# A decoder trunk on one core: a planner sets the order on every engine, transposing transfers replace some of TensorE's transposes, and four more blocks per MLP layer use seven products

## The chip, the core and the metric

The kernel runs on one core of a Trainium2 chip. The core has engines with queues of their own, each served in order: TensorE (PE) multiplies matrices, VectorE (DVE), ScalarE (ACT) and GpSimd (POOL) work elementwise, SyncE (SP) issues most transfers. An instruction waits on semaphores for what it reads and for the buffer that it writes. The metric is device time in microseconds of one execution, as the median of several runs.

## The reference

Two layers on x of 256 tokens by 2048 features, all in float32: a retention layer, then a latent-attention (MLA) layer, each followed by a squared-ReLU MLP. Cut to what matters:

```python
def retention(h, w_in, w_out, cos, sin):            # 8 heads, q and k of 256, v and gate of 512 each
    q, k, v, gate = split(h @ w_in)
    ...                                             # rotary q, k; decayed scores and state; per-head norm of o
    return (jax.nn.silu(gate) * o) @ w_out

def sq_relu_mlp(h, w1, w2):                         # w1 2048 x 8192, w2 8192 x 2048
    return jnp.square(jax.nn.relu(h @ w1)) @ w2

for layer in range(2):
    h = rms_norm(x, norm_mix[layer])
    x = x + (retention(h, ...) if layer == 0 else mla_attention(h, ...))
    x = x + sq_relu_mlp(rms_norm(x, norm_mlp[layer]), mlp_w1[layer], mlp_w2[layer])
```

## The kernel before

**Three products for one.** PE multiplies in a fast format that keeps fewer bits than float32. So each operand is split into a high part (ACT casts, line 216) and a low part (DVE subtracts, line 217), and a product is three matmuls: high by high, high by low, low by high (lines 409 to 411), each 128x512.

**Blocks.** Weights come as blocks of 256 rows by 1024 columns, 1 MB each, named *raw*, with three buffers; SP issues a load when DVE has finished with the buffer (line 324). The parts go to the buffers *wh* and *wl* of 1024 columns, five of each. A plain block takes eight products. A block "by seven" takes seven, in the manner of Strassen: DVE makes three sums of the weights (lines 363, 372, 373) and ACT and DVE split these too; the activations' sums are made once per block of activations (`with_sums`). Which of a pair's eight blocks go by seven is a tuple in the code:

```python
SEVEN, LATE, ODD, HEAD = (3, 5, 7), (5, 7), (1, 3, 5, 7), (2, 4, 6, 7)
```

**Pairs and groups.** A "pair" (`gemm_pair`) is eight blocks against the same 1024 output columns. An MLP layer is four groups; a group is two pairs of W1 (p = 2g and 2g + 1) and two pairs of W2. In the trace u is W1's product and d is W2's. At the end of a W1 pair, `pair_out` copies the sums out of PSUM (ACT, line 432; DVE, lines 434 to 439), `summed` adds (line 448), ACT applies ReLU with the norm (line 877), and the result, tokens by features, must be turned to features by tokens for W2. PE does that by eight 128x128 transposes for each half of the pair against the identity in *cst* (line 235, *hid_tp*); ACT squares what comes out (line 886), and ACT and DVE split it. The retention layer turns each head's gated output y in the same way (*ytp*).

**What sets the order.** The Python code records instructions in an order written out by hand: a queue of deferred functions (`later`, counted in blocks) puts the turning of a pair among the blocks of the next. Manual rules (`queued_behind`) hold single DVE or POOL instructions behind others. Products of W2's earlier groups are added to x in HBM by accumulating transfers from POOL (`to_home`, line 152).

Of the kernel before, what the change touches and what calls it, by code (L numbers as in the profile page):

```python
# [14 lines left out]
I32 = mybir.dt.int32  # L15
AF = mybir.ActivationFunctionType
# [3 lines left out]


# [24 lines left out]
GROUPS = (4, 4, 4, 4)  # L46
SEVEN, LATE, ODD, HEAD = (3, 5, 7), (5, 7), (1, 3, 5, 7), (2, 4, 6, 7)
# [19 lines left out]
def yoco(ctx: ExitStack, tc: tile.TileContext, a):  # L67
    nc = tc.nc
# [3 lines left out]
    def f2k(shape, name, dtype=F32):  # L72
        return pool.tile([P, *shape], dtype, tag="f2k", bufs=14, name=name)

    def small(w, name):
        return pool.tile([P, w], F32, tag="small", bufs=36, name=name)
# [5 lines left out]
    def bank(tag, shape, name):  # L82
        t = psum.tile([P, 512], F32, tag=tag, bufs=4 if tag == "acc" else 2, name=name)
        return shaped(t, shape)

    def two_banks(name):
        return psum.tile([P, 2, 512], F32, tag="at", bufs=1, name=name)

    def act_tile(name, dtype=F32R):

        return pool.tile([P, 2, 2, S], dtype, tag="act", bufs=24, name=name)


    queue, low_part, first_low = [], [None], [None]
    clock, count, ahead = [0], itertools.count(), [None, None]
# [19 lines left out]
    gains = pool.tile([P, G_ALL], F32, name="gains")  # L115
    cst = pool.tile([P, C_ALL], F32, name="cst")
    pos_i = pool.tile([P, NT], I32, name="pos_i")
    gpe = pool.tile([P, 2 * ROPE], F32, name="gpe")
# [3 lines left out]
    neg_half = pool.tile([P, 16], F32, name="neg_half")  # L122
# [4 lines left out]
    zeros = pool.tile([P, 512], BF16, tag="junk", bufs=1, name="zeros")  # L127
# [6 lines left out]
    x_home = [[dram.tile([P, 512], F32, name=f"xh_{t}_{b}") for b in range(NB)] for t in range(NT)]  # L134
# [14 lines left out]
    def to_home(c, p):  # L149

        def send(t, j, i):
            ins = nc.gpsimd.dma_start(x_home[t][2 * p + j], c[t][j][i], accum_op=ALU.add)
            tc.add_manual_dep(
                ins.ins, low_part[0].ins.name,
                mybir.DependencyInfo(mybir.DependencyClass.Sync, mybir.DependencyReason.SCHED_ONLY), reason="spaced",
            )
# [8 lines left out]
    def sums_into_x(c, name):  # L165
# [6 lines left out]
        queued_behind(nc.vector.tensor_tensor(v, c["p6"], o["p1"], op=ALU.add), low_part[0])  # L172
        nc.vector.tensor_tensor(u, c["p7"], v, op=ALU.add)

        def join(*parts):
            for t, j, part, op in parts:
                queued_behind(nc.vector.tensor_tensor(x[t][j], x[t][j], part, op=op), low_part[0])
# [31 lines left out]
    def square_sum(src, acc, name):  # L209
        junk = pool.tile([P, 512], BF16, tag="junk", bufs=1, name=f"{name}_sq")  # L210
# [26 lines left out]

    def stream(w, chunk, cols, name, use, done=None, before=None):

        raw = pool.tile([P, 2048], F32, tag="raw", bufs=3, name=f"{name}_raw")  # L240
# [3 lines left out]
        for half in range(2):  # L244
            wh = pool.tile([P, 1024], F32R, tag="wh", bufs=5, name=f"{name}_wh{half}")
            wl = pool.tile([P, 1024], F32R, tag="wl", bufs=5, name=f"{name}_wl{half}")
# [68 lines left out]
    def queued_behind(ins, before):  # L315
        tc.add_manual_dep(
            ins.ins, before.ins.name,
            mybir.DependencyInfo(mybir.DependencyClass.NoSync, mybir.DependencyReason.DATA), reason="order",
        )

    def quad(w, chunk, x, mm, name, split_ends=False):

        raw = pool.tile([P, 2048], F32, tag="raw", bufs=3, name=f"{name}_raw")
# [9 lines left out]
        def parts(src, n, part, after=None):  # L333
            wh = pool.tile([P, 1024], F32R, tag="wh", bufs=5, name=f"{name}_wh{part}")
            wl = pool.tile([P, 1024], F32R, tag="wl", bufs=5, name=f"{name}_wl{part}")
            low = low_part[0] = split(wh[:, : n * 512], wl[:, : n * 512], src)
            if after is not None:
                queued_behind(low, after)
            if part == 0:
                first_low[0] = low  # L340
# [21 lines left out]
        u = [pool.tile([P, 2, 512], F32, tag="us", bufs=2, name=f"{name}_u{i}") for i in range(2)]  # L362
        first_sum = nc.vector.tensor_tensor(
# [3 lines left out]
        if first_low[0] is not None:  # L367
            queued_behind(first_sum, first_low[0])
        if ahead[1] is not None:
            queued_behind(first_sum, ahead[1])  # L370
            ahead[1] = None
        nc.vector.tensor_tensor(u[1][:, 0], u[0][:, 0], raw[:, 512:1024], op=ALU.add)
        summed_up = nc.vector.tensor_tensor(u[1][:, 1], u[1][:, 0], raw[:, 1536:], op=ALU.add)  # L373
        b11, b22 = parts(raw[:, 0:1024], 2, 0, summed_up)
        mm("p1", a(0, 0), b11)
        mm("c12", s(3), b22)
        (b21,) = parts(raw[:, 1536:], 1, 1, summed_up)
# [156 lines left out]
    def add_to_x(acc, b, ss, name):  # L534
        for t in range(NT):
            for part in acc[t] if isinstance(acc[t], tuple) else (acc[t],):
                added = nc.vector.tensor_tensor(x[t][b], part, x[t][b], op=ALU.add)
                if name == "n2" and b >= 2:
                    queued_behind(added, low_part[0])
# [19 lines left out]
    pos_f = pool.tile([P, NT], F32, name="pos_f")  # L559
# [733 lines left out]
```

## Time and profile before

| | us |
|---|---|
| median of 3 runs | 2460.17 (2459.62 to 2461.29) |
| span of the profiled execution, its own time | 2456.3 |
| PE busy | 2446.2 |
| DVE busy | 2212.2 |
| ACT busy | 1641.3 |
| POOL busy | 238.0 |

The profile records one execution, and its span runs from the first to the last instruction. The time of a run also holds what lies around the span. Matmuls overlap in the records (a 128x512 matmul is recorded as 389 ns and starts every 227 ns), so PE's busy time is read as "was anything running", and what a matmul costs is read from the distance of starts. A group row reads: line, engine, operation, what it writes and reads, count | busy us, mean ns | idle time just before, and what ended it.

### The profile page before, as it was taken

The page shows a single profiled execution, that of the slowest core. Times are in us where ns is not written, and L with a number is a line of the kernel's source. Part 1 is how long each engine was busy: PE and PEld are TensorE (multiplying, and loading weights), DVE is VectorE, ACT ScalarE, POOL GpSimd, SP SyncE. Part 2 cuts the span into 40 slices and gives each one's busy share as a digit, 9 for nine tenths or more (in the row PEclk, how much of TensorE's full clock was granted, in tenths as well). Part 3 has the DMA queues.
Part 4 walks back from the last instruction along what each step waited for, and adds up shares of the span by engine and source line. Part 5 has one row for each costly group of instructions (what it writes and reads, how often), then busy time and mean ns, then how long its engine had stood idle before and what let it go on. Part 6 is the DMA issues. An engine that isn't in the chain of part 4 may idle for free.

```text
span 2456.3 us, 31721 instructions
## 1 busy us (share of the span) xinstructions
PE 2446.2 (100%) x11614; PEld 2057.6 (84%) x11614; DVE 2212.2 (90%) x2919; ACT 1641.3 (67%) x2307; POOL 238.0 (10%) x287
## 2 busy tenths in 40 slices
PE   9999999999999999999999999999999999999999
PEld 7888888888888888888888888998888888888887
DVE  7899899888899999999999998777899999999998
ACT  6566666556676767667676777577667667676674
POOL 6400001000000010010110001101000100100100
PEclk9999999999999999999999999999999999999999
DMA  8555569556565586695786555444555865957854
GB/s 309 207 201 191 192 202 259 191 183 224 197 218 194 196 254 218 207 272 187 241 253 213 200 202 180 155 162 173 197 199 205 252 228 194 262 198 229 264 209 170
DMA packets 93692, 521.05 MB, mean 212 GB/s; under 512 B 11104, under 2 KB 12512, under 8 KB 40288
## 3 DMA queue, kind: packets, MB, share of 16 engines
q1 hardware_dynamic: 72144, 472.83, 55.2%
q0 software_dynamic: 21248, 46.15, 8.9%
q8 instruction: 91, 1.49, 0.2%
q14 instruction: 65, 0.53, 0.1%
q10 hardware_dynamic: 144, 0.05, 0.0%
HBM read 479.14 MB, written 39.85 MB: 211 GB/s over the span
## 4 chain that ended last, share of the span: by engine, by line
PE 92%; DVE 2%; ACT 1%; issue 0%; DMA 0%; POOL 0%; ACTq 0%; DVEq 0%
PE u_c L411 7%; PE u_c L410 7%; PE u_c L409 7%; PE d_c L411 6%; PE d_c L410 6%; PE d_c L409 6%; PE rp_c L411 3%; PE rp_c L409 3%; PE rp_c L410 3%; PE u_p L411 2%; PE u_p L410 2%; PE u_p L409 2%; PE rq_acc L307 2%; PE rk_acc L307 2%; PE ro_c L411 2%; PE ro_c L409 2%
## 5 line engine op out<-in xcount | busy, mean ns | idle before, releaser
L217 DVE TENSOR_TENSOR d_wl<-d_raw,d_wh 128x1024 fp32r<-128x1024 f32 (+1 forms) x256 | 278.7, 1111 | 31.6 <-ACT d_wh L216 31.6
L217 DVE TENSOR_TENSOR u_wl<-u_raw,u_wh 128x1024 fp32r<-128x1024 f32 (+1 forms) x256 | 279.3, 1113 | 29.8 <-ACT u_wh L216 29.8
L409 PE MATMUL u_c<-u_wh,n 128*128 128x512 f32 x712 | 278.3, 392 | 0.0
L411 PE MATMUL u_c<-u_wh,n 128*128 128x512 f32 x712 | 277.2, 389 | 0.0
L410 PE MATMUL u_c<-u_wl,n 128*128 128x512 f32 x712 | 277.2, 389 | 0.0
L409 PE MATMUL d_c<-d_wh,hid 128*128 128x512 f32 x706 | 275.4, 392 | 0.5 <-ACT d_wh L216 0.5
L411 PE MATMUL d_c<-d_wh,hid 128*128 128x512 f32 x706 | 275.0, 390 | 0.0
L410 PE MATMUL d_c<-d_wl,hid 128*128 128x512 f32 x706 | 274.8, 389 | 0.0
L216 ACT CAST u_wh<-u_raw 128x1024 fp32r<-128x1024 f32 (+1 forms) x256 | 241.3, 973 | 49.6 <-PE u_c L411 24.1
L216 ACT CAST d_wh<-d_raw 128x1024 fp32r<-128x1024 f32 (+1 forms) x256 | 240.3, 971 | 39.9 <-PE d_c L411 16.6
L216 ACT CAST d_wh<-d_u 128x1024 fp32r<-128x1024 f32 x106 | 108.1, 1051 | 119.7 <-DVE d_u L373 82.6
L216 ACT CAST u_wh<-u_u 128x1024 fp32r<-128x1024 f32 x104 | 106.2, 1052 | 116.0 <-DVE u_u L373 77.3
L411 PEld LDWEIGHTS u_c<-u_wh,n 128*128 128x128 f32 x712 | 133.7, 188 | 27.8
L410 PEld LDWEIGHTS u_c<-u_wl,n 128*128 128x128 f32 x712 | 133.8, 188 | 27.4 <-DVE u_wl L217 0.3
L409 PEld LDWEIGHTS u_c<-u_wh,n 128*128 128x128 f32 x712 | 133.7, 188 | 27.0
L409 PEld LDWEIGHTS d_c<-d_wh,hid 128*128 128x128 f32 x706 | 132.6, 188 | 28.2 <-ACT d_wh L216 1.4
L411 PEld LDWEIGHTS d_c<-d_wh,hid 128*128 128x128 f32 x706 | 132.5, 188 | 27.6
L410 PEld LDWEIGHTS d_c<-d_wl,hid 128*128 128x128 f32 x706 | 132.6, 188 | 27.5 <-DVE d_wl L217 0.4
L216 ACT CAST rp_wh<-rp_raw 128x1024 fp32r<-128x1024 f32 x112 | 103.8, 945 | 74.2 <-PE rp_c L411 49.2
L217 DVE TENSOR_TENSOR rp_wl<-rp_raw,rp_wh 128x1024 fp32r<-128x1024 f32 x112 | 119.7, 1090 | 16.4 <-ACT rp_wh L216 16.2
L217 DVE TENSOR_TENSOR u_wl<-u_u,u_wh 128x1024 fp32r<-128x1024 f32 x104 | 123.5, 1222 | 3.1 <-ACT u_wh L216 2.8
L217 DVE TENSOR_TENSOR d_wl<-d_u,d_wh 128x1024 fp32r<-128x1024 f32 x106 | 125.8, 1221 | 0.0
(570 smaller groups left out, 6505.3 us busy)
## 6 DMA issues: line engine op xcount, KB each, us to landing
u_raw<-in_mlp_w SPq DMA_DIRECT2D x128, 1024.0 KB, 5.4
d_raw<-in_mlp_w SPq DMA_DIRECT2D x128, 1024.0 KB, 4.9
rp_raw<-in_ret_w_gv SPq DMA_DIRECT2D x56, 1024.0 KB, 4.8
ro_raw<-in_ret_w_out SPq DMA_DIRECT2D x32, 1024.0 KB, 4.9
uq_raw<-in_mla_w_uq SPq DMA_DIRECT2D x24, 768.0 KB, 4.3
rq_raw<-in_ret_w_qk SPq DMA_DIRECT2D x16, 1024.0 KB, 4.9
rk_raw<-in_ret_w_qk SPq DMA_DIRECT2D x16, 1024.0 KB, 4.8
xh<-d_c POOLq DMA_DIRECT2D x48, 256.0 KB, 6.1
```

Of the source, the lines that this page charges most:

```text
L216: nc.scalar.copy(h, src)
L217: return nc.vector.tensor_tensor(l, src, h.bitcast(F32), op=ALU.subtract)
L307: nc.tensor.matmul(acc[f], wh[:, cols], a.rearrange("p i s -> p (i s)"), start=k == 0, stop=k == nk - 1)
L409: nc.tensor.matmul(dst, ah, bh, start=n == 0, stop=False)
L410: nc.tensor.matmul(dst, ah, bl, start=False, stop=False)
L411: nc.tensor.matmul(dst, al, bh, start=False, stop=n == total[key] - 1)
```

## The change

**The order.** `nc` is no longer the real engine interface but a `Plan`: calls are recorded, with their buffers as index sets, and nothing is emitted. At the end `emit` runs `schedule`, a list scheduler. It gives each recorded instruction a cost from tables in the code, a due time from what depends on it, and then plays the engines forward: of the instructions that are ready on an engine, the one with the earliest due time goes next. Buffer slots are handed out in that play too. The instructions are emitted in that order, on all five engines. All `queued_behind` rules go.

**The turning.** For the first pair of each two (even p) and for seven of eight heads' y, PE no longer transposes. ACT copies each float32 tile into two 16-bit halves (`_h`), SP issues four transposing transfers of 128 x 512 halves, and ACT writes the halves back interleaved (`joined`) before squaring and splitting as before. The second pair (odd p) and head 7 are still turned on PE.

**The blocks.** W1's odd pairs take four of eight blocks by seven (ODD), where they took three (SEVEN). The other tuples are as they were.

The diff, cut to its core:

```diff
--- before.py
+++ after.py
...
+class Plan:
+
+    ENGINES = {"tensor": "PE", "vector": "DVE", "scalar": "ACT", "gpsimd": "POOL", "sync": "SP"}
+    LATENCY = {"PE": 55, "DVE": 36, "ACT": 48, "POOL": 110, "SP": 60}
...
+        op.engine, op.method, op.args, op.kw = self.ENGINES[engine], (engine, method), args, kw
+        op.number, op.before, op.after, op.new = len(self.ops), {}, [], []
+        op.made = op.held = None
+        op.behind, op.ahead = set(), []
...
+    def time(self, op, outs, ins):
+        engine, (_, method) = op.engine, op.method
+        n = max(v.index.size for v in outs if isinstance(v, View)) if any(isinstance(v, View) for v in outs) else 0
+        m = max([n] + [v.index.size for v in ins])
+        op.moves = None
+        if "dma" in method:
+            size = max(n, m) * P * (2 if "transpose" in method else 4)
+            issue = {"SP": 380, "ACT": 100, "POOL": 870}[engine]
+            if "transpose" in method:
+                issue = 1290
+            rate, wait = (208, 3200) if op.kw.get("accum_op") is not None else (349, 3000 if engine == "POOL" else 1800)
...
+            if "transpose" in method:
+                rate, wait = 180, 2200
+            op.moves = (size / rate, wait)
+            return issue, issue
...
+            if not op.after:
+                op.due = -whole
...
+            at, e = best
+            if not ready[e]:
+                while waiting[e] and waiting[e][0][0] <= at:
+                    _, _, op = heapq.heappop(waiting[e])
+                    heapq.heappush(ready[e], (op.due, op.number, op))
+            _, _, op = heapq.heappop(ready[e])
...
+        order = self.schedule()
+        with self.tc.manual_schedule(engines=engines):
+            for op in order:
+                engine, method = op.method
+                fn = getattr(getattr(self.nc, engine), method)
+                op.made = fn(*(real(v) for v in op.args), **{k: real(v) for k, v in op.kw.items()})
...
+TURNED_Y = 7
+STEPS = (((3,3,4),(3,4,5)),(None,None))
+TURNS = ((0,1),(0,1))
...
-    nc = tc.nc
+    nc = Plan(tc.nc, tc)
...
+    def halves_of(v):
+        return v.bitcast(U16).rearrange("p (n two) -> p two n", two=2)
+
+    def turn_by_dma(blocks, name, steps, then):
+
+        parts = [f2k([2, 512], f"{name}_h{t}", U16) for t in range(NT)]
+        for t in range(NT):
+            nc.scalar.copy(parts[t], halves_of(blocks[t]))
+
+        def turn():
+            turned = [f2k([4, S], f"{name}_t{i}", U16) for i in range(2)]
+            for t in range(NT):
+                for i in range(2):
+                    nc.sync.dma_start_transpose(turned[i][:, :, t * P : (t + 1) * P], parts[t][:, i])
+            for k2 in range(2):
+                later(steps[1 + k2] - steps[0], lambda k2=k2: then(turned, k2))
+
+        later(steps[0], turn)
+
+    def joined(turned, k2, u):
+
+        for i in range(2):
+            dst = halves_of(u.rearrange("p j s -> p (j s)"))[:, i]
+            part = nc.scalar.copy(dst, turned[i][:, 2 * k2 : 2 * k2 + 2].rearrange("p j s -> p (j s)"))
...
-                if ahead[0] is not None:
-                    queued_behind(low_part[0], ahead[0])
-                    ahead[0] = None
...
-    def queued_behind(ins, before):
-        tc.add_manual_dep(
-            ins.ins, before.ins.name,
-            mybir.DependencyInfo(mybir.DependencyClass.NoSync, mybir.DependencyReason.DATA), reason="order",
-        )
...
+            y_act.append((yt, with_sums(src, f"y{h}{k2}") if summed_up else None))
+
+        def join(turned, k2):
+            u = f2k([2, S], f"yu{h}{k2}")
+            joined(turned, k2, u)
+            split_up(k2, u)
+
         def turn():
+            if h < TURNED_Y:
+                turn_by_dma(ys, f"y{h}", (3,5,7), join)
+                return
             for k2 in range(2):
                 tp = transposed(lambda t, j: ys[t][:, (2 * k2 + j) * P : (2 * k2 + j + 1) * P], f"ytp{h}{k2}")
-                yt = act_tile(f"y{h}{k2}")
-                more = None
-                if len(y_act) in (HEAD if h < RH // 2 else LATE):
-                    u = f2k([2, S], f"yu{h}{k2}")
-                    nc.scalar.copy(u, tp)
-                    split_act(yt, u)
-                    more = with_sums(u, f"y{h}{k2}")
-                else:
-                    split_act(yt, tp)
-                y_act.append((yt, more))
+                u = f2k([2, S], f"yu{h}{k2}")
+                nc.scalar.copy(u, tp)
+                split_up(k2, u)
 
         later(2 if h else 3, turn)
 
...
         w1, w2 = a[f"mlp_w1_{layer}"], a[f"mlp_w2_{layer}"]
         f0 = 0
         for gi, nf in enumerate(GROUPS):
-            hid, blocks = [], []
+            blocks = []
             last = gi == len(GROUPS) - 1
 
-            def up(c, p, hid=hid, blocks=blocks):
+            def up(c, p, blocks=blocks):
 
                 need(r, NT)
                 c = summed(c)
-                for t in range(NT):
-                    for i in range(2):
-                        nc.scalar.activation(c[t][i], c[t][i], AF.Relu, scale=r[t])
-
-                def turn(i):
-                    for q in (2 * i, 2 * i + 1):
-                        name = f"hid{layer}_{p}{q}"
-                        tp = transposed(
-                            lambda t, j: c[t][q // 2][:, (q % 2 * 2 + j) * P : (q % 2 * 2 + j + 1) * P], f"{name}_tp"
-                        )
+
+                def turn_on_pe(i):
+                    for k2 in range(2):
+                        name = f"hid{layer}_{p}{2 * i + k2}"
+                        tp = transposed(lambda t, j: c[t][i][:, (k2 * 2 + j) * P : (k2 * 2 + j + 1) * P], f"{name}_tp")
                         u = f2k([2, S], f"{name}_u")
                         nc.scalar.activation(u, tp, AF.Square)
-                        v = act_tile(name)
-                        split_act(v, u)
-                        blocks.append((v, with_sums(u, name) if len(blocks) in ODD else None))
-                        hid.append(v)
-
-                later(0, lambda: turn(0))
-                later(1, lambda: turn(1))
+                        split_up(u, name)
+
+                def turn(i):
+                    for t in range(NT):
+                        nc.scalar.activation(c[t][i], c[t][i], AF.Relu, scale=r[t])
+                    steps = STEPS[p % 2][i]
+                    if steps is None:
+                        turn_on_pe(i)
+                        return
+                    turn_by_dma(
+                        [c[t][i] for t in range(NT)], f"hid{layer}_{p}{i}", steps,
+                        lambda turned, k2: square(turned, i, k2),
+                    )
+
+                def square(turned, i, k2):
+                    name = f"hid{layer}_{p}{2 * i + k2}"
+                    u = f2k([2, S], f"{name}_u")
+                    joined(turned, k2, u)
+                    nc.scalar.activation(u, u, AF.Square)
+                    split_up(u, name)
+
+                def split_up(u, name):
+                    v = act_tile(name)
+                    split_act(v, u)
+                    entry = [v, None]
+                    blocks.append(entry)
+                    if len(blocks) - 1 in ODD:
+                        later(0.5, lambda: entry.__setitem__(1, with_sums(u, name)))
+
+                for i in range(2):
+                    later(TURNS[p % 2][i], lambda i=i: turn(i))
 
             for p in range(f0 // 2, (f0 + nf) // 2):
-                seven = SEVEN if p % 2 else ODD if p else LATE
+                seven = (ODD, ODD)[p % 2] if p else LATE
                 gemm_pair(
                     w1, p * 8, act, [i in seven for i in range(8)], f"u{layer}_{p}", lambda c, p=p, up=up: up(c, p)
                 )
@@ -917,7 +1355,7 @@
                 def add(c, p=p, last=last):
                     into_x(done, c, p, 1) if last else to_home(c, p)
 
-                kinds = [i in ((LATE if last else ODD) if p else SEVEN) for i in range(2 * nf)]
+                kinds = [i in ((LATE if last else (SEVEN, ODD)[1]) if p else (SEVEN, ODD)[0]) for i in range(2 * nf)]
                 gemm_pair(w2, p * 32 + 2 * f0, blocks, kinds, f"d{layer}_{gi}{p}", add)
             f0 += nf
 
...
+    nc.emit()
```

What the planner does with this is seen in the engines' queues. In names, u0_31 is layer 0, W1 pair 3, block 1; u0_2 is what pair 2 left; hid0_20 is the first block of hidden activations of pair 2; the last number is a buffer's.

PE, at the boundary of the first and second block of W1's pair 3 in layer 0. Before, with the first half of pair 2 turned there:

```order
L409 MATMUL u0_3_c22_8495<-u0_30_wh1_8499,n116_00_6305 128x512
L410 MATMUL u0_3_c22_8495<-u0_30_wl1_8500,n116_00_6305 128x512
L411 MATMUL u0_3_c22_8495<-u0_30_wh1_8499,n116_00_6305 128x512
L235 MATMUL hid0_20_tp_8525<-cst_62,u0_2_c11_8464 128x128
L235 MATMUL hid0_20_tp_8525<-cst_62,u0_2_c21_8466 128x128
L235 MATMUL hid0_20_tp_8525<-cst_62,u0_2_c11_8464 128x128
L235 MATMUL hid0_20_tp_8525<-cst_62,u0_2_c21_8466 128x128
L235 MATMUL hid0_21_tp_8535<-cst_62,u0_2_c11_8464 128x128
L235 MATMUL hid0_21_tp_8535<-cst_62,u0_2_c21_8466 128x128
```

In the changed kernel:

```order
L421 MATMUL u0_3_c22_8568<-u0_30_wh1_8518,n116_00_6380 128x512
L421 MATMUL u0_3_c22_8568<-u0_30_wl1_8532,n116_00_6380 128x512
L421 MATMUL u0_3_c22_8568<-u0_30_wh1_8518,n116_00_6380 128x512
L421 MATMUL u0_3_p1_8598<-u0_31_wh0_8539,n116_01_6404 128x512
L421 MATMUL u0_3_p1_8598<-u0_31_wl0_8551,n116_01_6404 128x512
L421 MATMUL u0_3_p1_8598<-u0_31_wh0_8539,n116_01_6404 128x512
L421 MATMUL u0_3_c12_8562<-u0_31_wh0_8539,n101_more_6462 128x512
L421 MATMUL u0_3_c12_8562<-u0_31_wl0_8551,n101_more_6462 128x512
L421 MATMUL u0_3_c12_8562<-u0_31_wh0_8539,n101_more_6462 128x512
```

The eight transposes (two tiles of four) are gone, and block 1 starts with the product p1 of a block by seven, where it started with c11 of a plain one.

ACT, in blocks 3 to 5 of the same pair of the changed kernel, from the ReLU of pair 2's first half to the first copies out of its turned halves (`_wh` are casts of weights, `_t0` the turned 16-bit tile):

```order
L421 ACTIVATE u0_2_c21_8529<-u0_2_c21_8529,n1_r_6870 128x512
L421 COPY hid0_20_h0_8679<-u0_2_c11_8524 128x1024
L421 COPY hid0_20_h1_8687<-u0_2_c21_8529 128x1024
L421 CAST u0_34_wh0_8697<-u0_34_raw_8575 128x1024
L421 CAST u0_34_wh1_8706<-u0_34_raw_8575 128x1024
L421 CAST u0_35_wh0_8718<-u0_35_raw_8639 128x1024
L421 CAST u0_35_wh1_8726<-u0_35_raw_8639 128x512
L421 COPY hid0_20_u_8741<-hid0_20_t0_8690 128x512
L421 COPY hid0_21_u_8747<-hid0_20_t0_8690 128x512
L421 CAST u0_35_wh2_8754<-u0_35_u1_8708 128x1024
L421 CAST u0_35_wh3_8764<-u0_35_u0_8692 128x1024
L421 COPY hid0_20_u_8741<-hid0_20_t1_8715 128x512
```

Before, ACT took the turned tile from PSUM with one squaring instruction for each block:

```order
L877 ACTIVATE u0_2_c22_8460<-u0_2_c22_8460,n1_r_6762 128x512
L886 ACTIVATE hid0_20_u_8530<-hid0_20_tp_8525 128x512
L886 ACTIVATE hid0_21_u_8540<-hid0_21_tp_8535 128x512
L216 CAST hid0_20_8532<-hid0_20_u_8530 128x2x256
L216 CAST hid0_21_8542<-hid0_21_u_8540 128x2x256
```

The two 16-bit copies and four copies back are new; four casts of weights stand between the last 16-bit copy and the first copy back.

SP, in the same place of the changed kernel:

```order
L421 DMA u0_35_raw_8639<-in_mlp_w1_0 128x2048
L421 DMA u0_36_raw_8657<-in_mlp_w1_0 128x2048
L421 DMA_TRANSPOSE hid0_20_t0_8690<-hid0_20_h0_8679 128x4x128
L421 DMA_TRANSPOSE hid0_20_t0_8690<-hid0_20_h1_8687 128x4x128
L421 DMA_TRANSPOSE hid0_20_t1_8715<-hid0_20_h0_8679 128x4x128
L421 DMA_TRANSPOSE hid0_20_t1_8715<-hid0_20_h1_8687 128x4x128
L421 DMA u0_37_raw_8738<-in_mlp_w1_0 128x2048
L421 DMA d0_100_raw_8759<-in_mlp_w2_0 128x2048
L421 DMA d0_101_raw_8820<-in_mlp_w2_0 128x2048
```

Before, the same loads followed each other:

```order
L324 DMA u0_35_raw_8728<-in_mlp_w1_0 128x2048
L324 DMA u0_36_raw_8772<-in_mlp_w1_0 128x2048
L324 DMA u0_37_raw_8806<-in_mlp_w1_0 128x2048
L324 DMA d0_100_raw_8866<-in_mlp_w2_0 128x2048
L324 DMA d0_101_raw_8941<-in_mlp_w2_0 128x2048
```

Four transposing transfers now stand between the loads of blocks 6 and 7.

At the start of the program SP's first transfer was of the activations; in the changed kernel it is that of the constants (*cst*, 128x672), which stood fifteenth:

```order
L421 DMA cst_69<-in_cst 128x672
L421 DMA rg00_raw_73<-in_ret_w_gv0 128x512
L421 DMA x0t_0_77<-in_xt 128x256
L421 DMA rg00_raw_73<-in_ret_w_gv0 128x512
L421 DMA x0t_0_77<-in_xt 128x256
```

Before:

```order
L648 DMA x0t_0_99<-in_xt 128x256
L253 DMA rg00_raw_105<-in_ret_w_gv0 128x512
L656 DMA x0t_0_99<-in_xt 128x256
L253 DMA rg00_raw_105<-in_ret_w_gv0 128x512 x2
L654 DMA x0t_1_135<-in_xt 128x512
```

The loads of the first weights and activations now stand behind it.

More of the change, by code (lines that the diff above doesn't have):

```diff
@@ L331, in s, with parts @@
             return [more[:, n // 2, i, n % 2 * P : (n % 2 + 1) * P] for i in range(2)]
[L333 to L340, printed above, removed]
+        def parts(src, n, part):
+            wh = nc.tile(pool, [P, 1024], F32R, f"{name}_wh{part}", "wh", 5)
+            wl = nc.tile(pool, [P, 1024], F32R, f"{name}_wl{part}", "wl", 5)
+            low_part[0] = split(wh[:, : n * 512], wl[:, : n * 512], src)
             return [[i[:, j * 512 : (j + 1) * 512] for i in (wh, wl)] for j in range(n)]
```

437 lines of the change are left out of this document (378 added, 59 removed).

## The prediction

> **What bounds the kernel now.** I read the page first: the span, the engines' busy times and the shares of the chain that ended last.
>
> ```profile
> span 2456.3 us, 31721 instructions
> PE 2446.2 (100%) x11614; PEld 2057.6 (84%) x11614; DVE 2212.2 (90%) x2919; ACT 1641.3 (67%) x2307; POOL 238.0 (10%) x287
> PE 92%; DVE 2%; ACT 1%; issue 0%; DMA 0%; POOL 0%; ACTq 0%; DVEq 0%
> ```
>
> TensorE (PE) is busy for all but 2456.3 - 2446.2 = 10.1 us and carries 92% of the chain. VectorE (DVE) is second, 90%. The table of stretches then says where PE's idle time lies, and what DVE has left; its columns are stretch, length, and busy time with instructions of PE, PEld, DVE, ACT and POOL, then clock, DMA share and GB/s.
>
> ```profile
> 0.00:20.00 20.00, 17.88 (x65) 11.45 (x66) 11.63 (x23) 13.15 (x24) 2.06 (x8) 1.00 0.87 289
> 248.90:316.50 67.60, 67.60 (x334) 57.07 (x334) 61.81 (x83) 42.86 (x57) 1.82 (x4) 1.00 0.53 180
> 939.11:1107.27 168.16, 168.16 (x761) 139.62 (x759) 156.95 (x183) 114.22 (x145) 13.82 (x16) 1.00 0.72 225
> 1343.00:1484.00 141.00, 139.66 (x708) 118.04 (x707) 131.04 (x194) 104.19 (x180) 8.43 (x11) 1.00 0.57 200
> 2328.07:2456.30 128.23, 123.22 (x557) 101.40 (x555) 119.47 (x147) 77.22 (x100) 2.14 (x4) 1.00 0.54 189
> ```
>
> The third row is one whole MLP group (two pairs of W1, two of W2): PE is never idle, DVE sits idle 168.16 - 156.95 = 11.2 us, ACT 53.9 us. A retention head (second row) looks the same with more room: DVE idle 5.8 of 67.6 us. PE's idle time is at the ends (2.1 us in the first row, 5.0 in the last) and 1.3 us between the layers (fourth row). So an instruction taken off PE shortens the run by its own time, as long as DVE stays below PE.
>
> **What leaves PE.** Matmuls overlap in the trace, so I take distances between starts.
>
> ```profile
> 1991.13 0.39 PE L410 MATMUL u_c<-u_wl,n 128*128 128x512 f32 x1
> 1991.36 0.39 PE L411 MATMUL u_c<-u_wh,n 128*128 128x512 f32 x1
> 1991.59 1.03 PE L235 MATMUL hid_tp<-cst,u_c 128*128 128x128 f32 x8
> 1992.38 0.48 PE L409 MATMUL u_c<-u_wh,n 128*128 128x512 f32 x1
> 1992.69 0.40 PE L410 MATMUL u_c<-u_wl,n 128*128 128x512 f32 x1
> ```
>
> 512-column matmuls follow one another at 0.227 us. From 1991.36 to 1992.69 are 1.33 us for two such steps (0.45) and eight transposes: a run of eight costs 0.88 us.
>
> ```profile
> L235 PE MATMUL hid_tp<-cst,u_c 128*128 128x128 f32 x256 | 33.1, 272 | 0.0
> L235 PE MATMUL ytp<-cst,y 128*128 128x128 f32 x64 | 8.5, 273 | 0.5 <-DVE y L764 0.5
> ```
>
> Of the 256 hid_tp transposes, those of the even pairs go, 128, or 16 runs; of the 64 ytp, those of seven heads, 56, or 7 runs. 23 x 0.88 = **20.3 us**. One more block by seven products saves a product of three matmuls; four odd pairs in two layers make eight blocks: 8 x 3 x 0.227 = **5.4 us**. Together 25.7 us.
>
> **What the seven-product blocks ask of DVE.** Each needs the three sums (one of 1024 columns, two of 512) and one low part of 1024 and one of 512 beyond a plain block. Back to back, DVE starts follow each other so:
>
> ```profile
> 935.34 1.21 DVE L217 TENSOR_TENSOR u_wl<-u_raw,u_wh 128x1024 fp32r<-128x1024 f32 x1
> 936.47 0.69 DVE L438 TENSOR_TENSOR u_v<-u_p,u_v 128x512 f32<-128x512 f32 x1
> 937.08 0.69 DVE L448 TENSOR_TENSOR u_c<-u_c,u_u 128x512 f32<-128x512 f32 x1
> ```
>
> 1.13 us for 1024 columns, 0.61 for 512: 2 x 1.13 + 3 x 0.61 = 4.1 us a block, one block a group. The group shrinks on PE by two runs of eight and one product, 2 x 0.88 + 0.68 = 2.4 us, to 165.7. DVE would have 156.95 + 4.1 = 161.1 us in it, 97%, and 4.7 us idle instead of 11.2. It fits, closely; I cost it at nothing, and the cover is that 4.7 us. Without it each us is paid once in each of eight groups.
>
> **What the transposing transfers ask.** Per half of a pair ACT copies two tiles into 16-bit halves (128x1024) and later writes four pieces of 512 back; squaring and splitting stay. The trace has no such copy; the nearest rows are these.
>
> ```profile
> L216 ACT CAST u_wh<-u_raw 128x1024 fp32r<-128x1024 f32 x204 | 210.8, 1062 | 45.7 <-PE u_c L411 21.3 <-ACT u_wh L216 14.8 <-DMA u_raw<-in_mlp_w 5.9
> L216 ACT CAST u_wh<-u_raw 128x512 fp32r<-128x512 f32 x52 | 32.6, 627 | 3.8 <-PE u_c L411 2.8
> ```
>
> At 1.06 and 0.63 us a group gets 4 x 1.06 + 8 x 0.63 + 1.7 for the extra block (1.06 + 0.63) = 11 us, against ACT's 53.9 us idle. Strided halves could double the copies (20 us) or, being half the bytes, cost half (6); the idle time hides all three, so nothing is charged for ACT's work itself. Its order can still make it wait: rival B.
>
> Four transfers of 128 KB per half, 184 in all, go into SP's queue between weight loads. Their issue and landing are unknown. The nearest rows:
>
> ```profile
> 1.18 0.42 SPq L253 DMA_DIRECT2D rg_raw<-in_ret_w_gv  x1
> SPq L324 <- DVE u_wl L217: 620.7, 127, 11.0
> u_raw<-in_mlp_w SPq DMA_DIRECT2D x128, 1024.0 KB, 5.4
> dec<-in_decay SPq DMA_DIRECT2D x8, 128.0 KB, 4.9
> x0t<-in_xt SPq DMA_DIRECT2D x2, 128.0 KB, 2.9
> DMA packets 93692, 521.05 MB, mean 212 GB/s; under 512 B 11104, under 2 KB 12512, under 8 KB 40288
> ```
>
> A plain issue holds SP 0.42 us; SP waits 620.7/127 = 4.9 us for DVE before each W1 load. So four issues fit up to 1.2 us each, three times the row. A 128 KB transfer lands in 2.9 to 4.9 us; I take 4.9, since these too stand beside 1 MB loads. The bytes, 24 MB beside 521 MB, are small, and DMA is at 0.72 in the group. What is left is waits: from nothing to the prices of the rivals.
>
> **The new order as a whole.** At most it removes PE's idle time inside the run: 10.1 less the start and end, about 3 us; the tail (last matmul, add, store) stays. Against it, the constants (336 KB) now go first in SP's queue: one issue, 0.42, and up to 0.344 MB / 289 GB/s = 1.2 us before the first matmul; bounds 0 to 1.6, I take 1.0, because the same bytes came a little later before. For small new stalls at 23 places I take 2 us (bounds -3 and the rivals' prices), nearer to the row of 11.2 us idle, in which none reached PE, than to a full loss.
>
> **Sum.** 2456.3 - 20.3 - 5.4 + 1.0 + 2.0 = 2433.6 us of span. The span is 3.9 us under the median of the runs (2460.17), which I add: **2437 us**, 0.9% faster; its own range is 2429 to 2447.
>
> **Rivals.**
> A, *VectorE takes over as the bound; slower.* DVE's 11.2 us of idle time a group might be needed, since each low part waits for its cast and its load. If all of it stays, a group takes 161.1 + 11.2 = 172.3 instead of 165.7 us: 8 x 6.6 = 53 us, 2490 us. It decides from 4.7 us of needed idle time, and cancels the gain at about 7.6.  For it: 97% on a queue served in order. Against it: these rows, which say that casts waited for PE to release buffers 76 and 67 times, so the idle time is mostly a full pipeline.
>
> ```profile
> ACT u_wh L216 <- PE u_c L411: 62.6, 76, 3.5
> ACT d_wh L216 <- PE d_c L411: 53.6, 67, 3.5
> ```
>
> B, *the turned halves land late and ACT stands still.* In the new order ACT has four weight casts, 3 x 1.06 + 0.63 = 3.8 us, between the second 16-bit copy of a pair's first half and the copy that waits for its transfers; weight casts queue behind that copy, DVE behind them, and PE has about one block (5.1 us) in hand. At 4.9 us nothing shows. Each us of landing above 8.9 costs a us at eight places; the gain is gone at 12, and 13 us would give 2437 + 8 x 4.1 = 2470. For it: no row has such a transfer. Against: second halves have some 12 us of casts in between, and a 1 MB load lands in 5.4 us.
>
> [...]
>
> C, *the order also recovers PE's idle time:* no new stall, 3 us less inside: 2437 - 2 - 3 - 1 = 2431 us. Against: the order was not the cause of most of that idle time; the sums behind the last products were.
>
> D, *the gain is given back by many small waits:* A at about 7.6 us and B at 12 meet at 2460.
>
> **Chances.** Forecast 0.65, C 0.14, D 0.07, A 0.08, B 0.06. A change of 0.2% (5 us) is about what can be told from none: faster 0.65 + 0.14 = 0.79, within 0.2% 0.07 (D), slower 0.08 + 0.06 = 0.14. The range leaves out A, B and half of D above and the best of C below: 2427 to 2462.
>
> **What would show it.** PE's rows should have 128 hid_tp and 8 ytp, and a full MLP group should take 165.7 us with PE's idle time at 0. DVE's busy time should rise by 8 x 4.1 = 33 us, ACT's by about 120 (46 x 1.06 + 92 x 0.63 + 8 x 1.7). A is right if PE waits for low parts in the odd pairs, B if ACT's waits name the turned tiles for more than a few us each and PE's gaps follow. Wrong on PE's side would be a run of eight that saves less than 0.88 us.

## The result and the profile after

The changed kernel takes 2481.74 us (median; 2479.39 to 2483.38) beside 2460.73 us of the kernel before in the same session: a ratio of 1.0085, 95% interval 1.0071 to 1.0099. It is slower by 21 us, where the prediction had 23 us faster.

The page of the changed kernel, the lines that answer to the first ones of before:

```profile
span 2477.6 us, 31762 instructions
PE 2465.7 (100%) x11406; PEld 2035.9 (82%) x11406; DVE 2240.7 (90%) x2959; ACT 1739.1 (70%) x2457; POOL 248.1 (10%) x287
PE 96%; DVE 2%; DMA 1%; ACT 1%; issue 1%; SPq 0%; DVEq 0%; ACTq 0%
```

TensorE has 208 instructions less (11406 against 11614), is idle for 11.9 us (10.1 before) and carries 96% of the chain. So no new wait took the gain. Less work, hardly more idle time, and yet 20 us more busy: the work itself must have become slower. The stretches of the changed kernel (columns as in the prediction: stretch, length, PE, PEld, DVE, ACT, POOL, clock, DMA share, GB/s) are the start, one whole MLP group, and 90 us of W1's and W2's products in which all of PE's instructions are 128x512 matmuls:

```profile
0.00:20.00 20.00, 17.90 (x61) 12.20 (x62) 12.56 (x24) 14.23 (x27) 0.30 (x5) 1.00 0.91 320
987.60:1157.20 169.60, 169.60 (x741) 137.41 (x740) 160.99 (x188) 123.58 (x160) 13.82 (x16) 1.00 0.78 230
840.00:930.00 90.00, 90.00 (x391) 72.92 (x390) 85.96 (x96) 55.56 (x66) 13.01 (x15) 1.00 0.84 241
```

The last stretch in the kernel before:

```profile
840.00:930.00 90.00, 90.00 (x399) 74.55 (x398) 82.09 (x88) 55.32 (x66) 13.34 (x16) 1.00 0.84 245
```

Both are busy for all 90 us at a granted clock of 1.00, but 391 matmuls run in the changed kernel and 399 in the one before. Over the whole trace the distance from one 128x512 matmul's start to the next start has a median of 232 ns and a mean of 233.4 in the changed kernel, 227 and 228.9 before. With 9412 of them that is 4.5 x 9412 = 42 us, which turns a gain of some 20 us into a loss of 21. The pace is slower in every stage but one (the retention layer's q and k products), with and without transposing transfers nearby, and the narrower matmuls (384 and 256 columns) kept theirs within 1 ns. The MLP group took 169.6 us instead of the forecast 165.7.

### The profile page after: what moved, and what is told of

The parts are those of the page before. It is cut to its first block, busy times and chain, and to the rows that moved or that the text cites. A ratio compares the mean times of both kernels' runs of the same rounds, so it can differ in the third digit from the quotient of the medians.

```text
span 2477.6 us, 31762 instructions
## 1 busy us (share of the span) xinstructions
PE 2465.7 (100%) x11406; PEld 2035.9 (82%) x11406; DVE 2240.7 (90%) x2959; ACT 1739.1 (70%) x2457; POOL 248.1 (10%) x287
## 2 busy tenths in 40 slices
DMA packets 143742, 533.12 MB, mean 215 GB/s; under 512 B 61152, under 2 KB 62560, under 8 KB 90336
## 4 chain that ended last, share of the span: by engine, by line
PE 96%; DVE 2%; DMA 1%; ACT 1%; issue 1%; SPq 0%; DVEq 0%; ACTq 0%
PE d_c L421 20%; PE u_c L421 20%; PE rp_c L421 8%; PE u_p L421 7%; PE ro_c L421 6%; PE d_p L421 6%; PE uq_acc L421 4%; PE rk_acc L421 4%; PE rq_acc L421 4%; PE rp_p L421 3%; PE ku_acc L421 2%; PE wo_acc L421 2%; PE ro_p L421 1%; PE wop_c L421 1%; PE dqp_c L421 1%; PE rg_acc L421 1%
## 5 line engine op out<-in xcount | busy, mean ns | idle before, releaser
L421 PE MATMUL d_c<-d_wh,hid 128*128 128x512 f32 x1412 | 464.4, 396 | 0.0
L421 PE MATMUL u_c<-u_wh,n 128*128 128x512 f32 x1328 | 435.6, 394 | 0.0
L421 PEld LDWEIGHTS u_c<-u_wh,n 128*128 128x128 f32 x1328 | 249.3, 188 | 58.2
L421 PE MATMUL u_c<-u_wl,n 128*128 128x512 f32 x664 | 261.7, 394 | 1.0 <-DVE u_wl L421 1.0
L421 ACT CAST u_wh<-u_u 128x1024 fp32r<-128x1024 f32 x120 | 123.7, 1051 | 97.1 <-DVE u_u L421 77.8
L421 PE MATMUL rp_c<-rp_wh,a 128*128 128x512 f32 x560 | 183.0, 393 | 0.0
L421 DVE TENSOR_TENSOR u_wl<-u_u,u_wh 128x1024 fp32r<-128x1024 f32 x120 | 143.9, 1221 | 23.8 <-ACT u_wh L421 23.8
L421 PEld LDWEIGHTS rp_c<-rp_wh,a 128*128 128x128 f32 x560 | 105.1, 188 | 24.8 <-DVE rk_u L421 0.9
L421 PE MATMUL u_p<-u_wh,n_more 128*128 128x512 f32 x360 | 122.6, 395 | 0.0
L421 PE MATMUL ro_c<-ro_wh,y 128*128 128x512 f32 x368 | 120.0, 396 | 0.0
```

The costliest lines, as they stand in the source:

```text
L421: op.made = fn(*(real(v) for v in op.args), **{k: real(v) for k, v in op.kw.items()})
```

## Experiments: where the pace comes from

What differs everywhere is where buffers lie in SBUF, the on-chip memory that the engines read. Places are given modulo 256, the remainder of a buffer's start in bytes divided by 256. In the kernel before, `pool.tile(tag=..., bufs=N)` places all N buffers of a kind side by side, and the ten weight halves (*wh* and *wl*), the 24 buffers of split activations (*act*) and the three landing buffers of the weights (*raw*) all start at 192 over a multiple of 256. In the changed kernel every slot has a tag of its own and is placed when the planned order first needs it, among 32-byte tiles: the weight halves start at 32 (four) or 64 (six) modulo 256, the act buffers at 0, 32, 64, 96, 128 or 192. In the changed kernel's trace, runs of matmuls whose two operands start equal modulo 256 have a median of 227 ns (both at 32, both at 64), all other pairings 229 to 234. That is a correlation in one trace; the runs below change the places alone.

**The changed kernel with the large buffers placed alike.** Same instructions in the same order on all engines; small tiles are placed first:

```diff
         order = self.schedule()
+        for buf in self.first:                 # gains, pos_i, pos_f, gqn
+            buf.get()
+        for i in range(36):
+            self.pool.tile([P, 8], F32, name=f"small_{i}", tag=f"small{i}", bufs=1)
```

> The changed kernel, every instruction in the same order on every engine; only the places in SBUF differ. In the changed kernel a large buffer is placed when the planned order first needs it, among the 32-byte ones, so that 5 of 10 weight-half buffers, the three landing buffers and 9 of 24 act buffers start at an address that is 32 over a multiple of 64; in the kernel before all of these start at a multiple of 64. Here the small ones are placed first, and all large ones start at multiples of 64. Between the two traces the start-to-start time of the 128x512 matmul went from 228.9 to 233.4 ns (9412 of them: 42 us) and nothing else of that size changed. Theory PLACES (the start address sets the pace): 227 ns median again, 2481.7 - 42 = 2440 us, from 2434 to 2445. Rival TRAFFIC (the transposing transfers, the 16-bit copies or the busier DVE take the reads away from PE): pace stays at 232, 2482 us. Rival ORDER (the planned order or its waits slow the matmuls): the same, 2482 us.

(The changed kernel has four, not five, of the ten halves and eight, not nine, act buffers 32 over a multiple of 64.) Measured: 2444.98 us (2439.81 to 2448.99), ratio to before 0.9936, interval 0.9918 to 0.9955. The same stretch:

```profile
840.00:930.00 90.00, 90.00 (x399) 74.53 (x398) 86.32 (x97) 55.43 (x67) 13.89 (x16) 1.00 0.90 255
```

The pace is 227 ns again, with every transfer, copy and wait of the change in place. Traffic and order are out as causes of the slow pace. Some 37 us go with the places alone, where the pace gives 42; most of the rest is one stall of 4.7 us in this run that the changed kernel does not have (described with the transfers of y below). This version is faster than both kernels.

**The kernel before, with places moved.** One tile is widened by 32 bytes, or one or a few other tiles are placed later, so that the kinds of buffers move against each other; the order of all engines stays:

```diff
-    pos_i = pool.tile([P, NT], I32, name="pos_i")             # everything 32 further on
+    pos_i = pool.tile([P, 16], I32, name="pos_i")[:, :NT]
...
+MOVED = (("pos_f", NT, "act"), ("gqn", 1, "us"))               # act buffers 32 past the halves
```

> The kernel before, with one 32-byte buffer made 64 bytes wide ahead of the others, so that every large buffer (raw, weight halves, act, fused-load, float tiles) starts 32 over a multiple of 64; nothing else. PLACES: pace 233 to 235 ns instead of 227, so 2461 + 9436 x 5 to 7 ns = 2508 to 2527 us, and DVE, ACT copies and landings perhaps longer too. TRAFFIC and ORDER: 2461 us, pace 227.

> The kernel before, with two 32-byte buffers moved so that only the ten weight-half buffers (the operand that moves through the array) start 32 over a multiple of 64. In the changed kernel's trace a matmul with only its moving operand off took 233.5 ns on average, with only its standing one off 233.8, with neither 231.4. PLACES: the moving operand costs at least 2 ns of pace, 2461 + 9436 x 2 = 2480 us, up to 2510 if it is the whole of it. If it is the standing operand alone, or the traffic of others: 2461 us.

> The kernel before, with only the 24 act buffers (the standing operands, the tables and the norms' tiles) 32 over a multiple of 64. PLACES: from the same rows 2 to 2.5 ns a matmul, 2480 us; 2461 us if only the moving operand counts. What this and the run with the halves add up to, beside the run with everything off, says whether the landing buffers and float tiles matter too.

> The kernel before, with only the three landing buffers of the weights 32 over a multiple of 64; halves and act buffers as before. If what slows the matmul is that its two operands start at different places of a 64-byte line, nothing changes: pace 227 ns, 2460 us. If any traffic at other places slows it (VectorE and ScalarE read these buffers all the time), the pace rises to 229 or more, 2480 us.

> The kernel before, with two 32-byte buffers moved so that the act buffers (standing operands) start 64 bytes further on against the weight halves (moving operands); all at the same place of a 64-byte line. If only the 64-byte line counts: pace 227 ns, 2460 us. If the two starts must agree over a wider period (the changed kernel's matmuls that agreed at 64 but not at 128 or 256 were slow, 229 to 233 ns, those that agreed at 256 took 227): 229 to 233 ns, 2480 to 2520 us.

> The same with the act buffers 128 over (modulo 256) against the weight halves. If starts must agree at 128 only: pace 227, 2460 us. If at 256: about 232 to 233 ns, as the matmuls 128 apart in the changed kernel's trace, 2510 us.

> The same with the act buffers 256 over (modulo 512) against the weight halves. If starts must agree at 256: pace 227, 2460 us. If at 512: about 233 ns, 2510 us.

| what is moved | act against halves, modulo 256 | instructions in 840 to 930 us | us |
|---|---|---|---|
| nothing | 0 | 399 | 2459.65 (2460.06 beside the landing buffers, 2459.47 beside the last three) |
| everything by 32 | 0 | 399 | 2460.09 (ratio 1.0000, 0.9991 to 1.0009) |
| landing buffers by 32 | 0 | 399 | 2458.95, one run |
| halves by 32 | 32 | 388 | 2509.28 (1.0201, 1.0186 to 1.0216) |
| act by 32 | 32 | 388 | 2509.70 (1.0201, 1.0185 to 1.0216) |
| act by 64 | 64 | 388 | 2512.93, one run |
| act by 128 | 128 | 389 | 2506.76, one run |
| act by 256 | 0 | 399 | 2459.30, one run |

What is placed earlier moves too, so the second column, and not the first, says what the matmuls see. With "halves by 32" the landing buffers start at 128, the halves at 160 and act at 192; with "act by 32" they start at 128, 128 and 160. So act starts 32 past the halves in both.

The row of the stretch with everything moved by 32:

```profile
840.00:930.00 90.00, 90.00 (x399) 74.53 (x398) 82.69 (x89) 55.51 (x66) 13.03 (x15) 1.00 0.84 245
```

With the halves moved by 32:

```profile
840.00:930.00 90.00, 90.00 (x388) 72.45 (x387) 82.12 (x89) 55.46 (x65) 10.44 (x12) 1.00 0.77 232
```

With the act buffers moved by 64 and, below it, by 256:

```profile
840.00:930.00 90.00, 90.00 (x388) 72.50 (x387) 82.50 (x91) 55.67 (x66) 10.43 (x12) 1.00 0.75 226
```

```profile
840.00:930.00 90.00, 90.00 (x399) 74.53 (x398) 83.50 (x89) 55.82 (x65) 13.00 (x15) 1.00 0.84 248
```

My first form of the theory fell with the first of them: a start that is no multiple of 64 bytes costs nothing when both operands are off alike (2460.09 us, not 2508 to 2527). It is the difference between the two that counts: the weight halves (the operand that moves through the array) against the act buffers (the standing one). Equal modulo 256: 227 ns. Act 32, 64 or 128 past the halves: 233 ns, 47 to 53 us a run. Whether the halves or the act buffers are the ones off a multiple of 64 makes no difference (2509.28 and 2509.70 us), and where the landing buffers lie, which VectorE, ScalarE and DMA use all the time, costs nothing (2458.95 us). Act 32 short of the halves (224) was not run by itself; in the changed kernel's trace such pairings have a median of 234 ns. The run at 256 (2459.30 us) shows that the period is 256 and not 512. The last three rows and that of the landing buffers are single runs; steps of 50 us are far beyond the 4 us over which the unmoved kernel's times spread.

## Experiments: the terms of the sum, with the places alike

**The order alone.** Everything turned on TensorE, three blocks by seven, so the work of the kernel before in the planned order: `TURNED_Y = 0`, `STEPS = ((None,None),(None,None))`, `seven = (ODD, SEVEN)[p % 2]`.

> The planner alone, with the large buffers placed alike: everything turned on TensorE, odd pairs with three blocks by seven, so the same work as the kernel before in the planned order. The prediction charged the order with 1.0 us at the start and 2.0 us in small stalls that belong to the transfers: 2461 to 2464 us. If the order itself causes the stalls that keep the run with everything at 2445 instead of 2434 to 2437, it is 2469 to 2472; if they come from the transfers and the fourth block, 2461.

Measured 2459.19 us, ratio 0.9996 (0.9987 to 1.0005). The order of five engines, written by a planner, is worth the same as the hand-written one; its one cost that was found, a first product 1.4 us later, must be won back elsewhere; where was not followed.

**Three blocks by seven instead of four, transfers kept.** `seven = (ODD, SEVEN)[p % 2]`.

> The changed kernel with the large buffers placed alike, transposing transfers kept, and W1's odd pairs with three blocks by seven instead of four. The prediction's step: 24 matmuls at 0.227 us come back, 2445.0 + 5.4 = 2450 us, as long as VectorE (2241 us busy with four) has cover. Rival: VectorE is so close to the bound that the fourth block costs in waits what it saves: 2445 us, or below.

Measured 2449.57 us (ratio 0.9956, 0.9942 to 0.9970): the fourth block saves 4.6 us by the medians, where 5.4 was forecast. The runs of both versions spread over 9 us, so this agrees with the forecast but hardly shows it. The transfers as a whole save 2459.2 - 2449.6 = 9.6 us by the medians, give or take some 4, and not 20.3.

**Hidden tiles by transfers, y on TensorE.** `TURNED_Y = 0`.

> The changed kernel with large buffers placed alike (2445.0 us), hidden tiles turned by transfers, but the seven heads' y turned on TensorE. In the run with places alike the retention layer's last product starts no earlier than in the kernel before (first W1 product at 722.3 against 721.3 us), though 7 runs of eight had left it. If the step holds and the planned order lost it elsewhere in the layer, the 7 runs come back: 2445.0 + 7 x 0.76 = 2450 us. If the transfers of y cost there what they save (their landing took 5.7 us, against 2.8 for the hidden tiles, and DMA stands at 0.95), no change: 2445 us, or below.

Measured 2445.62 us (0.9945, 0.9928 to 0.9962), against 2444.98 with y turned by transfers: seven runs of eight transposes came back to TensorE and cost nothing that can be told, in times that spread over 5 and 9 us. In the profile of the run with the transfers, the gain of the layer is lost in one piece, 4.7 us at a weight load that landed 10 us after its issue (the layer ends 0.95 us later than in the kernel before):

```profile
395.00:402.00 7.00, 6.63 (x30) 5.16 (x28) 3.07 (x4) 3.58 (x4) 0.00 (x0) 1.00 0.86 273
402.00:406.00 4.00, 1.45 (x4) 1.23 (x5) 3.83 (x4) 1.57 (x2) 0.86 (x1) 0.86 0.05 23
406.00:412.00 6.00, 6.00 (x23) 4.78 (x23) 5.49 (x7) 2.10 (x2) 0.86 (x1) 0.81 0.78 176
```

TensorE waits for a low part, VectorE for the load (4.0 us in its waits), and then TensorE runs at a granted clock of 0.81 for some microseconds: the next eight matmuls start 0.43 us apart. Without the transfers of y the same 20 us have no such gap:

```profile
390.00:410.00 20.00, 19.55 (x86) 15.51 (x85) 18.17 (x21) 10.40 (x12) 2.64 (x4) 1.00 0.76 206
```

The kernel with the order alone stands 1.6 us there, the one with three blocks 3.8 us; DMA's share from 390 to 400 us was 0.95 to 0.96 in the kernel before, with the order alone, and here. That the transfers of y (landing 5.7 us in this run) are what makes the load late was not tested by itself. In the kernel with three blocks the clock did not fall, though TensorE stood longer at once, 3.6 us:

```profile
402.00:406.20 4.20, 0.58 (x4) 0.16 (x2) 2.38 (x3) 1.56 (x2) 0.00 (x0) 1.00 0.23 93
406.20:412.00 5.80, 5.59 (x23) 4.32 (x24) 5.80 (x7) 2.10 (x2) 1.73 (x2) 1.00 0.58 93
```

**Everything turned on TensorE, four blocks.** `TURNED_Y = 0`, `STEPS = ((None,None),(None,None))`; and the same with the second pair's turning recorded one block later, `TURNS = ((0,1),(1,2))`.

> The changed kernel with all large buffers at 64 over a multiple of 128 (as in the run that placed them so, 2445.0 us), but with every hidden and y tile turned on TensorE again: no transposing transfer, no 16-bit copy. If the prediction's step holds, 23 runs of eight come back at 0.88 us each: 2445.0 + 20.3 = 2465 us. The trace of the run with transfers has 184 transposes less, 14.9 us of start-to-start time with the stalls beside them, so a step that is lost in part would give 2458 to 2461. If the transfers cost nothing elsewhere, the difference is at least 18; if they delay weight loads and so stall TensorE, it is smaller than 15.

> The run with everything turned on TensorE and four blocks by seven in the odd pairs (2527.1 us), with the turning of the odd pairs recorded one block later. There TensorE stood 8 us a group, behind ACT's copies of the odd pair's sums, which ACT had queued behind weight casts that wait for TensorE. If that standstill is a matter of the place of the transposes in TensorE's order, a block (5.1 us) more of work ahead of them takes most of it: 2527 - 8 x 5 = 2487 us or less. If VectorE is the bound without the transfers, the time stays at 2520 to 2530.

Measured 2527.12 us (1.0280, 1.0261 to 1.0300) and 2522.44 (1.0252, 1.0231 to 1.0272). The fourth block, worth 4.6 us with the transfers, costs 68 us without them. One group of the first of them in the table of stretches:

```profile
1001.30:1177.10 175.80, 172.38 (x755) 141.40 (x755) 159.59 (x186) 113.48 (x144) 13.85 (x16) 0.97 0.68 215
```

The waits of the whole run (engine and what it made, whom it waited for, us in total, times, longest):

```profile
ACT d_wh L428 <- PE d_c L428: 97.8, 58, 7.8
DVE d_wl L428 <- ACT d_wh L428: 48.1, 22, 5.3
DVE d_u L428 <- DMA d_raw<-in_mlp_w: 36.9, 20, 3.3
PE hid_tp L428 <- ACT u_p L428: 16.0, 8, 2.0
PE d_c L428 <- ACT u_c L428: 13.0, 8, 1.6
```

I read this as a ring: TensorE waits for ACT's copies of the pair's sums; ACT has these behind casts that wait for TensorE to release a buffer (up to 7.8 us at once); VectorE waits for the casts. VectorE is busy 159.6 of 175.8 us, so its load is not what ends the group. Of the 68 us, 45 are more idle time of TensorE than with the order alone (55.4 against 10.4 us). The other 23 are slower work: the granted clock over the run is 0.991, and 0.97 in this group, where it was 1.00 with the order alone, and 0.9% of 2525 us is 23 us. A block more between the pair and its transposes changed 5 us, not 40 (two runs, four of the other): my account of it (the place of the transposes in TensorE's order) fell, and which link would have to be cut stays open.

**The second pair turned by transfers too.** `STEPS = (((3,3,4),(3,4,5)),((1,1,2),(1,2,3)))`.

> The changed kernel with the large buffers placed alike (2445.0 us) and the second pair of each two turned by transposing transfers too: 16 more runs of eight leave TensorE, 128 transposes. In the run without transfers and the one with them 184 transposes were 17.5 us, 0.76 a run of eight. If the transfers (landing 2.8 us) are in time for the fifth block of W2, which needs them some 20 us after the pair's end: 2445 - 16 x 0.76 = 2433 us. Rival: the chain of copy, transfer, copy, square and split is too long there and TensorE stands at eight places: 2445 us or more.

Measured 2469.61 us (1.0041, 1.0026 to 1.0055), 25 us slower than with the second pairs on TensorE. The rival's condition held, and the cost was more than it said; TensorE's longest waits:

```profile
PE d_c L428 <- ACT hid L428: 20.1, 12, 2.9
PE d_p L428 <- ACT hid L428: 4.0, 8, 0.5
PE u_c L428 <- DVE u_wl L428: 3.8, 6, 1.5
```

The hidden tiles' transfers landed in 3.8 us instead of 2.8, and TensorE waits for the last link of the way through copy, transfer, copy, square and split: it is too long for a pair whose tiles are needed next.

## Why the prediction was wrong, by its steps

**The step that failed** is the durations under "What leaves PE": "512-column matmuls follow one another at 0.227 us". It was read from the trace of before and carried over to the changed kernel for all 9412 of them. There they follow at a median of 232 ns. The change to `tile`, one tag for each slot, stands in the diff, and I read it as bookkeeping. None of the four rivals had the pace in it: they were all waits, and TensorE waits as little as forecast. With the places alike the run is at 2445 us, at the upper end of the forecast's own range of 2429 to 2447. The sum does not hold term by term even there: the transposes were to give 20.3 us, and the transfers that replace them gave about 10.

**What bounds the kernel:** right. TensorE, before and after.

**Transposes off TensorE:** the count is right, 128 hid_tp stay.

```profile
L421 PE MATMUL hid_tp<-cst,u_c 128*128 128x128 f32 x128 | 16.8, 273 | 0.0
```

Of 0.88 us a run: the group was to take 165.7 us, and with the places alike it does:

```profile
978.20:1143.90 165.70, 165.70 (x740) 137.37 (x739) 159.85 (x188) 122.72 (x159) 13.86 (x16) 1.00 0.78 235
```

The seven runs of ytp (6.2 us of the 20.3) gave nothing that can be told, by the run with y on TensorE. (23 x 0.88 is 20.2; the prediction has 20.3.)

**VectorE as the next bound (rival A):** wrong, as forecast. The group was to have 161.1 us of VectorE; it has 160.99 in the changed kernel. In all VectorE has 28.5 us more; 33 were forecast. The run with four blocks and everything on TensorE shows that VectorE's idle time alone is not the cover: without the transfers the fourth block cost 68 us.

**ACT's copies and the transfers (rival B):** it did not come, and its prices were about right. The groups of the changed kernel, then its turned tile's instructions (ns, least, median, most), then its transfers with their median landing in us:

```profile
L421 ACT COPY hid_u<-hid_t 128x512 uint16<-128x512 uint16 x64 | 49.0, 783 | 2.9 <-DMA hid_t<-hid_h 2.9
...
L421 ACT COPY hid_h<-u_c 128x1024 uint16<-128x1024 uint16 x32 | 31.7, 1039 | 0.0
```

```profile
L421 SPq DMA_TRANSPOSE hid_t<-hid_h x64: 1188/1216/1894, 787.0 to 2381.5; - x64
```

```profile
hid_t<-hid_h SPq DMA_TRANSPOSE x64, 2.8
y_t<-y_h SPq DMA_TRANSPOSE x28, 5.6
```

1.04 us a 16-bit copy (1.06 assumed), 0.78 a copy back (0.63), 98 us of ACT in all (120). An issue holds SP for 1.2 us, the bound up to which it was to fit; landing is 2.8 and 5.6 us (4.9 taken). ACT waited 2.9 us for turned tiles in the MLPs over the whole run. There are 92 transfers; the prediction's "184 in all" was a slip. It doubled the bytes, 12 MB more in the trace (533.12 against 521.05) and not 24, but entered no term of the sum. A hidden tile's transfer landed no later than the plain ones of 128 KB (2.8 us, against 2.9 to 4.9 in the rows of before and 4.1 to 4.9 in the changed kernel's); y's, at 5.6 us, landed later, and an issue held SP longer, 1.2 us (1.3 for y) against 0.42.

**The start:** charged with 1.0 us; the first product starts at 6.1 instead of 4.9 us. Right.

**The 8 us between 2437 and 2445** (8.8 in the spans, 2433.6 and 2442.4), from the starts in the traces of before and of the run with the places alike: the retention layer loses 6.2 us against its terms (it ends 0.95 us later than before instead of 5.2 earlier), the two MLPs fall short by 2.7 and 3.9, mostly in their last two pairs of W2's products (88.7 and 90.6 us before, 90.9 and 93.1 now, the second to the end of the span), MLA gains 1.9 that no term had, and the 2.0 us charged for small stalls come off: 6.2 + 2.7 + 3.9 - 1.9 - 2.0 = 8.9. So the step on the order mis-sized what it charged for stalls, and mis-placed them: they lie in the retention layer and at the MLPs' ends, not at the 23 runs.

## What to carry to other kernels

When a kernel is bound by TensorE, look at the distance of starts of its commonest matmul first, before and after: 2% there outweighed every instruction that this change saved, and neither busy time nor waits nor the clock row shows it. When buffers get new tags, sizes or an allocation order, compare where both operands of the hot matmuls start, modulo 256; placing the small tiles first was a repair of a few lines and some 37 us. When a change has several parts, run each alone: here the order was worth nothing, the hidden tiles' transfers most of the gain, y's transfers nothing that could be told, and the fourth block about 5 us or minus 68, depending on the transfers.

## What the runs showed of the hardware

- A 128x512 float32 matmul whose moving and standing operand start equal modulo 256 bytes follows the one before at 227 ns; with the standing one 32, 64 or 128 past the moving one at 233 on average. Both operands moved together by 32 bytes change nothing (2460.09 us, 399 instructions in the stretch). Shown by the placements above. Why is not shown. With the landing buffers alone moved, which VectorE, ScalarE and DMA use, the pace stayed at 227 ns (399 in the stretch, one run), so in that run the place of what the other engines use did not set it.
- It is not "equal is best" as such. In the q and k products of the retention layer, where the weights stand, the activations move and 512- and 256-column matmuls alternate, the matmul after a wide one starts 235 ns later (median) with equal places in the kernel before and 228 with act or halves moved by 32. It is 231 with the landing buffers moved, where the places are equal too, so something else counts there that no run isolates. That is 512 of the 9436 matmuls, so the other form decides.
- In the run with the places alike, after 2.9 us without work, eight matmuls of TensorE started 0.43 us apart instead of 0.227, 8 x 0.43 = 3.4 us in all, with the granted clock at 0.86 from 402 to 406 us and at 0.81 from 406 to 412. In the run with three blocks TensorE stood 3.6 us and the clock stayed at 1.00. By these rows the length of the gap alone does not decide; what does is not shown. That late load cost 8 x 0.2 = 1.6 us beside the 3.1 us of the wait.
